# Order of the early loads and of two weight sums in a QKV projection by seven products

## The chip, the cores and the metric

The kernel runs on one core of a Trainium2 chip. The metric is the device time of one execution in microseconds, as the median over runs. TensorE (PE) multiplies, VectorE (DVE), ScalarE (ACT) and GpSimd (POOL) prepare operands and take results out of the PSUM banks, and SyncE (SP) and ACT issue the DMAs between HBM and SBUF.

## The reference

```python
batch, seq, hidden = 16, 512, 768
x: (16, 512, 768) float32          w_qkv: (768, 2304) float32

qkv = np.matmul(x, w_qkv)
q = qkv[..., :hidden]
k = qkv[..., hidden:2*hidden]
v = qkv[..., 2*hidden:]
return np.stack([q, k, v], axis=0).astype(np.float32)
```

So it is one product of 8192 x 768 by 768 x 2304, with its columns stored as three arrays.

## The kernel before

**Tiling.** The rows of x are taken in 32 pairs of two tiles of 128 rows, numbered from 0 ("pair 2" is the third). The 768 contracted elements are six slices of 128, in two halves of three. Of the 2304 columns, q = 0 covers the first 1024 in two blocks of 512 (c = 0, 1), q = 1 the last 1024 in the same way, and between them lies a remainder of 256. "Block (q, c)" is such a block of 512 columns of w; it is loaded in two halves of three slices (768 KB each).

**Two ways to multiply.** Pairs 0 and 1 are done plainly by `block` (L384): for each of four row tiles six bf16 products of 128x512 accumulate in a PSUM bank, and ACT evicts it (L408). Later pairs use, for each q, seven products on 2x2 blocks with sums of operands: `do(u, n)` (L220) does product n of the quad u = (pair, q); its matrix products stand in `product` (L201, matmuls at L212). Products 1 and 2 are bf16, on x itself; the others are f32, on sums. The sums of x are s (`sums_x`, L177, GpSimd) and the sums of w are t1 to t4 (`sum_w(q, n)`, L105, DVE instruction at L113): 6 uses t2, 5 uses t1, 7 uses t3, 4 uses t4, and 3 uses a rounded copy b22. A quad has a bank u.x for products 1, 6, 7 and 4 in turn, evicted by ACT after each (L226, L233, L239, L243), a bank u.z for 2 (added by DVE, L230), and a bank u.y for 5 and then 3 on top of it; DVE adds u.y to one quarter of the result after 5 and 7 (L240) and, with 3 in it, to another (L246). The remainder is plain: `rem` (L267, matmuls L262, eviction L272, store L273).

**Pair 2 is the transition.** For q = 0 it uses the seven products, for q = 1 the plain blocks, because the sums of w for q = 1 aren't ready: its tiles 4 and 5 of blocks (1, 0) and (1, 1) stand between the products of quad a = (2, 0). From pair 3 on, `two` (L275) interleaves two quads. The kernel has a schedule written by hand: every engine executes its instructions in the order of the program text.

**How x arrives.** For pairs 2 and later `load_group` (L124, DMA at L128) fetches a quarter, 192 KB; `load_x` (L119) issues four, two of them on SP and two on the queue given. DVE transposes the pair (`transpose`, L130, instruction at L132) into xf. From xf, ACT rounds pair 2 to bf16 by halves (`round_half`, L470, instruction at L472) and GpSimd later pairs (`round_x`, L173, L175); then GpSimd builds the sums s. There are three buffers for a loaded pair, two for xf, five for a quad's results and eight PSUM banks, each in rotation.

**The early loads.** SP issues, in this order: x of pairs 0 and 1, the blocks of w (0,0), remainder, (0,1), (1,0), (1,1) and two quarters of x of pair 2 (L363 to L367). Stores follow on the same queue when their results are evicted: the remainders (L273), then the quads of pairs 0 and 1 (L253, L254 for q = 0; L257, L258 for q = 1). ACT issues the other two quarters of pair 2 after block (0, 1) (L461). SP gets to x of pair 3 (L463) after the stores of the quads of q = 0. During each plain block ACT casts the next block's two halves (L380) between its evictions.

**The order around the change**, from block (1, 0) on:

```python
    block(1, 0, b1[1], halves(range(4)), cast_next(1, 1, bt1))
    load_x(3, nc.sync)
    ...
    sum_w(1, 1)
    transpose(2)
    ...
    block(1, 1, bt1, halves(range(4)), round_half)
    sums_x(2)
    transpose(3)
    round_x(3)
    sums_x(3)
    sum_w(1, 2)
```

Pair 2 follows (L480 to L498), with `b22[0]` (ACT, L483), sum 3 (L486) and sum 4 (L497). `t_1`, which holds t1 to t4 of q = 1, lies in the buffers of the loaded blocks (0, 0) and (0, 1); t3 and t4 take that of (0, 1), from which `b22[0]` is cast.

Of the kernel before, what the change touches and what calls it, by code (L numbers as in the profile page):

```python
# [10 lines left out]
def kernel(  # L11
# [20 lines left out]
    nc = tc.nc  # L32
    P = 128
# [6 lines left out]
    KH = KT // 2  # L40
    KC = K // 4
    NP = M // (2 * P)
    CB = 512
    REM = N3 - 4 * CB
    Q_OFF = (0, 2 * CB + REM)
    R_OFF = 2 * CB
    fp32 = mybir.dt.float32
    f32r = mybir.dt.float32r
    bf16 = mybir.dt.bfloat16
    ident = mybir.ActivationFunctionType.Identity  # L50
# [12 lines left out]
    st_pool = ctx.enter_context(tc.tile_pool(name="st", bufs=4))  # L63
# [15 lines left out]
    b22 = [w_pool.tile([P, KH, CB], f32r, name=f"b22_{q}") for q in range(2)]  # L79
# [7 lines left out]
    def load_w(dst, j0, nj, off, cols):  # L87
        rows = w_qkv.rearrange("(p j) n -> p j n", j=KT)
        nc.sync.dma_start(dst, rows[:, j0:j0 + nj, off:off + cols])  # L89

    stage = {}

    def load_blocks(q, c, nj=KH):
        if q == 0:
            t = tq_pool.tile([P, KT, CB], fp32, name="st0", tag="tq")
            for j in range(0, KT, nj):
                load_w(t[:, j:j + nj], j, nj, Q_OFF[q] + c * CB, CB)
            stage[q, 0, c], stage[q, 1, c] = t[:, :KH, :], t[:, KH:, :]
        else:
            for h in range(2):  # L100
                t = st_pool.tile([P, KH, CB], fp32, name="st1", tag="st")
                load_w(t[:], h * KH, KH, Q_OFF[q] + c * CB, CB)
                stage[q, h, c] = t[:]

    def sum_w(q, n):  # L105
        t1, t2, t3, t4 = ts[q]
        o, in0, in1 = {
            1: (t1, stage[q, 0, 1], stage[q, 0, 0]),
            2: (t2, stage[q, 1, 1], t1),
            3: (t3, stage[q, 1, 1], stage[q, 0, 1]),  # L110
            4: (t4, stage[q, 1, 0], t2),
        }[n]
        nc.vector.tensor_tensor(o, in0, in1, op=sub)  # L113
# [5 lines left out]
    def load_x(p, other):  # L119
        for n in range(2):  # L120
            for h in range(2):
                load_group(p, 2 * h + n, (nc.sync, other)[h])

    def load_group(p, i, eng):  # L124
        if p not in xin:
            xin[p] = xin_pool.tile([P, 2 * P // G, KC], fp32, name="xin")
        rows = x_flat[p * 2 * P:(p + 1) * 2 * P, :].rearrange("(g b) k -> b g k", b=G)
        eng.dma_start(xin[p][i * G:(i + 1) * G], rows[:, :, i * KC:(i + 1) * KC])  # L128
# [65 lines left out]
    def quad(p, q):  # L194
        u = Quad()
        u.p, u.q = p, q
        u.o = o_pool.tile([P, 2, 2 * CB], fp32, name="o", tag="o")
        u.x = u.y = u.z = None
        return u

    def product(u, n, ps, start):  # L201
        t1, t2, t3, t4 = ts[u.q]
        if n <= 2:
            h = (n - 1) * KH
            lhs = [xb[u.p][:, h + j, :P] for j in range(KH)]
            rhs = [b1[u.q][:, h + j, :] for j in range(KH)]
        else:
            k, t = {3: (4, b22[u.q][:]), 4: (0, t4), 5: (1, t1), 6: (2, t2), 7: (3, t3)}[n]
            lhs = [sr[u.p][:, k, j, :] for j in range(KH)]
            rhs = [t[:, j, :] for j in range(KH)]  # L210
        for j in range(KH):
            nc.tensor.matmul(  # L212
                ps[:], lhs[j], rhs[j],
                start=(start and j == 0), stop=(j == KH - 1), skip_group_check=True,
            )

    def bank():
        return ps_pool.tile([P, CB], fp32, name="ps")

    def do(u, n):  # L220
        c11, c12 = u.o[:, 0, :CB], u.o[:, 0, CB:]
        c21, c22 = u.o[:, 1, :CB], u.o[:, 1, CB:]
        if n == 1:
            u.x = bank()
            product(u, 1, u.x, True)
            nc.scalar.activation(c11, u.x[:], ident)  # L226
        elif n == 2:
            u.z = bank()
            product(u, 2, u.z, True)
            nc.vector.tensor_tensor(c11, c11, u.z[:], op=add)  # L230
        elif n == 6:
            product(u, 6, u.x, False)
            nc.scalar.activation(c12, u.x[:], ident)  # L233
        elif n == 5:
            u.y = bank()
            product(u, 5, u.y, True)
        elif n == 7:
            product(u, 7, u.x, False)
            nc.scalar.activation(c22, u.x[:], ident)  # L239
            nc.vector.tensor_tensor(c22, c22, u.y[:], op=add)  # L240
        elif n == 4:
            product(u, 4, u.x, False)
            nc.scalar.activation(c21, u.x[:], ident)  # L243
        elif n == 3:
            product(u, 3, u.y, False)
            nc.vector.tensor_tensor(c12, c12, u.y[:], op=add)  # L246

    def rows_of(s, p, lo, hi):
        return out_flat[s, p * 2 * P:(p + 1) * 2 * P, lo:hi].rearrange("(r m) n -> m r n", m=P)

    def store_quad(u):
        if u.q == 0:
            nc.sync.dma_start(rows_of(0, u.p, 0, H), u.o[:, :, :H])  # L253
            nc.sync.dma_start(rows_of(1, u.p, 0, 2 * CB - H), u.o[:, :, H:])  # L254
        else:
            part = 2 * H - Q_OFF[1]
            nc.sync.dma_start(rows_of(1, u.p, H - part, H), u.o[:, :, :part])  # L257
            nc.sync.dma_start(rows_of(2, u.p, 0, H), u.o[:, :, part:])  # L258
# [8 lines left out]
    def rem(p):  # L267
        ps = ps_pool.tile([P, 2, REM], fp32, name="ps")
        for r in range(2):
            rem_row(p, r, ps[:, r, :])  # L270
        o = or_pool.tile([P, 2, REM], fp32, name="orem")
        nc.scalar.activation(o[:], ps[:], ident)  # L272
        nc.sync.dma_start(rows_of(1, p, R_OFF - H, R_OFF - H + REM), o[:])  # L273
# [87 lines left out]
    for h in range(2):  # L361
        load_w(st_rem[:, h * KH:(h + 1) * KH], h * KH, KH, R_OFF, REM)
    load_blocks(0, 1, KH)  # L363
    load_blocks(1, 0)
    load_blocks(1, 1)
    for i in range(2):
        load_group(2, i, nc.sync)  # L367
    quads = [[quad(p, q) for p in range(NS)] for q in range(2)]

    def busy(n):  # L370
# [13 lines left out]
    def block(q, c, w, groups, cast_next):  # L384

        ps = {}
        for group in groups:
            if callable(group):  # L390
                group()
                continue
            js, tiles = group
            for n in tiles:
                p, r = divmod(n, 2)
                if n not in ps:
                    ps[n] = bank()
                for j in js:
                    nc.tensor.matmul(
                        ps[n][:], xb[p][:, j, r * P:(r + 1) * P], w[:, j, :],  # L400
                        start=(j == 0), stop=(j == KT - 1), skip_group_check=True,
                    )
                if KT - 1 not in js:
                    continue
                if r == 0:
                    cast_next(p)
                u = quads[q][p]
                nc.scalar.activation(u.o[:, r, c * CB:(c + 1) * CB], ps[n][:], ident)  # L408
                if c == 1 and r == 1:
                    store_quad(u)  # L410

    def halves(tiles):
        return [(range(h * KH, (h + 1) * KH), tiles) for h in range(2)]

    act, dve = nc.scalar, nc.vector
    def cast_next(q, c, w):
        return lambda p: p < 2 and cast(q, p, c, w, act)
# [39 lines left out]
    for n in range(1, 5):  # L457
        sum_w(0, n)
    block(0, 1, bt0, halves(range(4)), cast_next(1, 0, b1[1]))
    for i in range(2, 4):  # L460
        load_group(2, i, act)  # L461
    block(1, 0, b1[1], halves(range(4)), cast_next(1, 1, bt1))
    load_x(3, nc.sync)  # L463
    t_1 = [tq_pool.tile([P, 2, KH, CB], f32r, name=f"t_1{n}", tag="tq") for n in range(2)]
    ts[1] = [t_1[n // 2][:, n % 2] for n in range(4)]
    sum_w(1, 1)
# [13 lines left out]
    a = quad(2, 0)  # L480
    quads[1].append(quad(2, 1))
    do(a, 1)
    act.activation(b22[0][:], stage[0, 1, 1], ident)  # L483
    do(a, 2)
    rem(2)
    sum_w(1, 3)  # L486
    block(1, 0, b1[1], [(range(KT), (4, )), (range(KT), (5, ))], nothing)
    load_x(4, nc.sync)
    do(a, 6)
    do(a, 5)  # L490
    block(1, 1, bt1, [(range(KT), (4, ))], nothing)
    do(a, 7)
# [1 line left out]
    do(a, 4)  # L494
    do(a, 3)
    store_quad(a)
    sum_w(1, 4)  # L497
    act.activation(b22[1][:], stage[1, 1, 1], ident)  # L498

# [43 lines left out]
```

## Time and profile before

| | |
|---|---|
| median of 8 runs | 364.37 us (364.23 to 366.02) |
| the profiled execution | 364.35 us |
| its span, first to last instruction | 362.6 us |
| granted TensorE clock | 0.999 |
| TensorE busy | 352.3 us (97%) |
| DVE, ACT, POOL busy | 224.0, 186.4, 178.8 us |
| HBM traffic | 297 GB/s over the span |

The profile lists instructions by engine with the program's line, the result and the operands ("xf<-xin"), the count where equal ones are merged, and in brackets the idle time before them with what ended it. Starts are measured; the ends of matmuls are modelled, so a matmul's duration is best read from the distance of two starts. In the chain of waits, the work that ended last is followed back from the end; "DMA xin<-in_x_dram" there is the time from the issue of a load to its landing. All times are in us from the first instruction.

### The profile page before, as it was taken

How to read it: one execution, taken by the hardware profiler on the slowest of the kernel's cores; microseconds unless marked ns; L12 is line 12 of the kernel's file. 1: busy time of each engine (PE TensorE's matmuls, PEld its weight loads, DVE VectorE, ACT ScalarE, POOL GpSimd, SP SyncE). 2: the span in 40 equal slices, each digit the busy share in tenths (PEclk: the TensorE clock that was granted, in tenths of full speed). 3: DMA queues.
4: the chain of work that ended last, by engine and by line, in shares of the span. 5: the costliest groups of instructions: out<-in, count | busy, mean ns of one | idle time of the engine just before them, and what ended most of it. 6: DMA issues, size and time to landing. Idle time of an engine off the chain costs nothing.

```text
span 362.6 us, 5205 instructions
## 1 busy us (share of the span) xinstructions
PE 352.3 (97%) x1750; PEld 250.8 (69%) x1782; DVE 224.0 (62%) x233; ACT 186.4 (51%) x308; POOL 178.8 (49%) x185
## 2 busy tenths in 40 slices
PE   8998989999999999999999999999999999999995
PEld 4544467777777777777777777777777777777774
DVE  3583887655666755656765566765566675556643
ACT  4585754554545454454555454545454545554543
POOL 0003677466644456654446664445664445665420
PEclk9999999999999999999999999999999999999999
DMA  7999987888999999999999898898999999999867
GB/s 299 403 374 354 357 292 247 271 302 271 324 304 294 278 294 278 310 307 293 293 273 295 281 324 305 293 272 296 275 323 302 290 288 283 287 294 315 294 235 256
DMA packets 81450, 108.09 MB, mean 298 GB/s; under 512 B 4880, under 2 KB 61456, under 8 KB 81424
## 3 DMA queue, kind: packets, MB, share of 16 engines
q1 hardware_dynamic: 65472, 95.96, 81.0%
q10 hardware_dynamic: 15952, 11.80, 9.9%
q8 instruction: 14, 0.23, 0.3%
q14 instruction: 12, 0.10, 0.1%
HBM read 32.24 MB, written 75.50 MB: 297 GB/s over the span
## 4 chain that ended last, share of the span: by engine, by line
PE 85%; DMA 9%; issue 2%; DVE 1%; SPq 1%; ACT 1%; ACTq 0%; DVEq 0%
PE ps L212 75%; PE ps L262 10%; DMA st<-in_w_qkv_dram 5%; DMA xin<-in_x_dram 4%; DVE t L113 1%; SPq L128 1%; SPq L89 0%; ACT o L243 0%; ACTq L303 0%; SPq L143 0%; ACT b L380 0%; ACT orem L317 0%; DVE o L240 0%; DVE o L230 0%; ACTq L319 0%
## 5 line engine op out<-in xcount | busy, mean ns | idle before, releaser
L212 PE MATMUL ps<-t,s 128*128 128x512 f32 x708 | 177.7, 399 | 0.0
L212 PEld LDWEIGHTS ps<-t,s 128*128 128x128 f32 x708 | 133.0, 188 | 30.4
L175 POOL CAST xb<-xf 128x1536 bf16<-128x1536 f32 x29 | 43.8, 1510 | 133.2 <-DVE xf L132 133.2
L240 DVE TENSOR_TENSOR o<-o,ps 128x512 f32<-128x512 f32 x59 | 40.5, 687 | 91.1 <-ACT o L239 91.1
L132 DVE STREAM_TRANSPOSE xf<-xin 128x1536 f32<-128x1536 f32 x30 | 88.6, 2954 | 8.7 <-DMA xin<-in_x_dram 8.7
L212 PE MATMUL ps<-b,xb 128*128 128x512 bf16 x326 | 80.0, 379 | 3.2 <-ACT xb L472 1.2
L212 PEld LDWEIGHTS <-xb 128*128 128x128 bf16 x354 | 32.1, 98 | 38.1 <-issue 7.6
L239 ACT ACTIVATE o<-ps 128x512 f32<-128x512 f32 x59 | 35.3, 598 | 44.4 <-PE ps L212 44.3
L233 ACT ACTIVATE o<-ps 128x512 f32<-128x512 f32 x59 | 35.3, 598 | 42.2 <-PE ps L212 39.3
L246 DVE TENSOR_TENSOR o<-o,ps 128x512 f32<-128x512 f32 x59 | 40.5, 687 | 22.6 <-PE ps L212 21.4
L212 PE MATMUL ps<-b,s 128*128 128x512 f32 x177 | 49.6, 389 | 1.7 <-DVE o L240 1.7
L226 ACT ACTIVATE o<-ps 128x512 f32<-128x512 f32 x59 | 35.2, 597 | 25.1 <-DVE o L246 21.4
L243 ACT ACTIVATE o<-ps 128x512 f32<-128x512 f32 x59 | 35.3, 598 | 24.2 <-PE ps L212 21.3
L183 POOL TENSOR_TENSOR s<-xf 128x384 fp32r<-128x384 f32 x30 | 31.8, 1061 | 31.7 <-DVE xf L132 31.7
L262 PE MATMUL ps<-w_rem,xb 128*128 128x256 bf16 x384 | 47.2, 273 | 0.0
L262 PEld LDWEIGHTS <-xb 128*128 128x128 bf16 x384 | 37.4, 98 | 11.2 <-issue 0.5
L212 PEld LDWEIGHTS ps<-b,s 128*128 128x128 f32 x177 | 33.1, 188 | 9.0 <-issue 2.1
L230 DVE TENSOR_TENSOR o<-o,ps 128x512 f32<-128x512 f32 x59 | 37.2, 672 | 2.0 <-ACT o L226 1.3
L184 POOL TENSOR_TENSOR s<-s,xf 128x384 fp32r<-128x384 f32 x30 | 30.4, 1013 | 2.4
L187 POOL TENSOR_TENSOR s<-xf,s 128x384 fp32r<-128x384 f32 x30 | 30.4, 1013 | 0.0
L185 POOL TENSOR_TENSOR s<-xf 128x384 fp32r<-128x384 f32 x30 | 30.4, 1012 | 0.0
L272 ACT ACTIVATE orem<-ps 128x512 f32<-128x512 f32 x31 | 18.5, 598 | 20.1 <-PE ps L262 20.1
(35 smaller groups left out, 119.7 us busy)
## 6 DMA issues: line engine op xcount, KB each, us to landing
out_dram<-o SPq DMA_DIRECT2D x62, 768.0 KB, 4.6
out_dram<-o SPq DMA_DIRECT2D x65, 256.0 KB, 4.2
xin<-in_x_dram SPq DMA_DIRECT2D x64, 192.0 KB, 6.9
xin<-in_x_dram ACTq DMA_DIRECT2D x56, 192.0 KB, 4.5
out_dram<-orem SPq DMA_DIRECT2D x31, 256.0 KB, 5.8
st<-in_w_qkv_dram SPq DMA_DIRECT2D x6, 768.0 KB, 11.1
xin<-in_x_dram SPq DMA_DIRECT2D x2, 768.0 KB, 4.9
st<-in_w_qkv_dram SPq DMA_DIRECT2D x6, 256.0 KB, 6.0
```

Source lines behind the costliest of these rows:

```text
L132: nc.vector.transpose(t[:].rearrange("p j (g b) -> p g j b", b=G), xin.pop(p)[:].rearrange("p g (a j) -> p g j a", a=G),)
L175: nc.gpsimd.tensor_copy(out=xb[p][:], in_=xf[p][:])
L183: g.tensor_tensor(s[:, 1], a21, a22, op=add)
L212: nc.tensor.matmul(ps[:], lhs[j], rhs[j], start=(start and j == 0), stop=(j == KH - 1), skip_group_check=True,)
L226: nc.scalar.activation(c11, u.x[:], ident)
L230: nc.vector.tensor_tensor(c11, c11, u.z[:], op=add)
L233: nc.scalar.activation(c12, u.x[:], ident)
L239: nc.scalar.activation(c22, u.x[:], ident)
L240: nc.vector.tensor_tensor(c22, c22, u.y[:], op=add)
L243: nc.scalar.activation(c21, u.x[:], ident)
L246: nc.vector.tensor_tensor(c12, c12, u.y[:], op=add)
L262: nc.tensor.matmul(ps, xb[p][:, j, r * P:(r + 1) * P], w_rem[j // KH][:, j % KH, :], start=(j == 0), stop=(j == KT - 1), skip_group_check= ...
```

## The change

Three things are reordered; nothing is computed differently and no DMA changes its size.

- On SP, the four quarters of x of pair 2 come after the first half of block (1, 1) and ahead of its last half, all four on SP; the two that ACT issued are gone from ACT. The four quarters of pair 3 follow the last half of w, ahead of all stores.
- On DVE, sum 3 of q = 1 goes from its place ahead of pair 2's additions L240 and L246 to behind them, next to sum 4 and ahead of the transpose of pair 4. (Sum 4 keeps its place.)
- On ACT, the cast to `b22[0]` goes from behind product 1 of pair 2 to behind its product 6.

```diff
             for h in range(2):
-                t = st_pool.tile([P, KH, CB], fp32, name="st1", tag="st")
-                load_w(t[:], h * KH, KH, Q_OFF[q] + c * CB, CB)
-                stage[q, h, c] = t[:]
+                load_half(q, h, c)
+
+    def load_half(q, h, c):
+        t = st_pool.tile([P, KH, CB], fp32, name="st1", tag="st")
+        load_w(t[:], h * KH, KH, Q_OFF[q] + c * CB, CB)
+        stage[q, h, c] = t[:]
...
     load_blocks(1, 0)
-    load_blocks(1, 1)
-    for i in range(2):
-        load_group(2, i, nc.sync)
+    load_half(1, 0, 1)
+    load_x(2, nc.sync)
+    load_half(1, 1, 1)
+    load_x(3, nc.sync)
...
     block(0, 1, bt0, halves(range(4)), cast_next(1, 0, b1[1]))
-    for i in range(2, 4):
-        load_group(2, i, act)
     block(1, 0, b1[1], halves(range(4)), cast_next(1, 1, bt1))
-    load_x(3, nc.sync)
...
     do(a, 1)
-    act.activation(b22[0][:], stage[0, 1, 1], ident)
     do(a, 2)
     rem(2)
-    sum_w(1, 3)
     block(1, 0, b1[1], [(range(KT), (4, )), (range(KT), (5, ))], nothing)
     load_x(4, nc.sync)
     do(a, 6)
+    act.activation(b22[0][:], stage[0, 1, 1], ident)
     do(a, 5)
...
     store_quad(a)
+    sum_w(1, 3)
     sum_w(1, 4)
     act.activation(b22[1][:], stage[1, 1, 1], ident)
```

## The prediction

> **What bounds the kernel now.** First the engine table: TensorE is the bound of the whole.
>
> ```profile
> PE 352.3 (97%) x1750; PEld 250.8 (69%) x1782; DVE 224.0 (62%) x233; ACT 186.4 (51%) x308; POOL 178.8 (49%) x185
> ```
>
> So only TensorE's idle time can be won. I asked the waits of PE between 26 and 60 us, where the change lies, and then the timeline of PE there:
>
> ```profile
> PE ps L212 <- DVE o L240: 1.7, 1, 1.7
> PE ps L212 <- ACT xb L472: 1.2, 1, 1.2
> ```
> ```profile
> 27.19 5.34 PE L399 MATMUL ps<-bt,xb 128*128 128x512 bf16 x23
> 33.77 1.47 PE L212 MATMUL ps<-b,xb 128*128 128x512 bf16 x6 [1.24 <-ACT xb L472]
> 46.23 0.93 PE L212 MATMUL ps<-b,s 128*128 128x512 f32 x3 [1.70 <-DVE o L240]
> 47.00 1.47 PE L212 MATMUL ps<-b,xb 128*128 128x512 bf16 x6
> 57.98 1.24 PE L212 MATMUL ps<-b,xb 128*128 128x512 bf16 x5
> ```
>
> Ends are modelled, so I go by starts. The plain products take 0.216 us each (24 from 22.01 to 27.19), the f32 ones 0.227 (three in 0.68), a remainder of 12 is 1.31. Block (1,1), started at 27.19, could hand over at 27.19 + 5.18 = 32.37; pair 2 starts at 33.77: **1.40 lost**, waiting for its rounded x. Pair 2 with its two extra tiles is 30 x 0.216 + 1.31 + 15 x 0.227 = 11.19, so pair 3 could start at 44.96; it starts at 47.00: **2.04 lost**. Pair 3 lasts 10.76 (its successor's first record is missing, so 57.98 less 0.22 = 57.76), like every later pair (10.74). So 3.4 us is all there is.
>
> Who makes them late: the chain of waits, then DVE's timeline.
>
> ```profile
> 22.65 7.06 DMA xin<-in_x_dram
> 32.06 5.68 DMA xin<-in_x_dram
> 40.81 1.73 DVE t L113
> 42.54 0.60 DVE o L230
> 43.14 2.34 DVE t L113
> 45.48 0.61 DVE o L240
> ```
> ```profile
> 29.90 2.93 DVE L132 STREAM_TRANSPOSE xf<-xin 128x1536 f32<-128x1536 f32 x1 [3.69 <-DMA xin<-in_x_dram]
> 37.87 3.03 DVE L132 STREAM_TRANSPOSE xf<-xin 128x1536 f32<-128x1536 f32 x1 [5.03 <-DMA xin<-in_x_dram]
> ```
>
> Both losses begin with x. Pair 2's x lands at 29.7, is transposed to 32.83, rounded to 33.7. Pair 3's lands at 37.8, because its loads sit on SP behind four stores (SP reaches them at 29.77); DVE then waits 5 us with pair 2's sums behind that transpose, and the additions of L230 and L240 behind those sums. L240 must finish before do(a, 3) may add to the same bank.
>
> **The change, part by part.**
>
> *x of pair 2 ahead of the last half block of w.* Four loads of 192 KB now follow the first half of block (1,1), which lands at 23.7 (SP's L253 waits for it until its issue at 23.71). The DMA engines are full, so bytes set the time:
>
> ```profile
> 13.50:18.50 5.00, 5.00 (x37) 3.41 (x35) 2.80 (x3) 3.27 (x7) 0.00 (x0) 1.00 1.05 407
> 42.50:45.00 2.50, 2.03 (x10) 0.96 (x7) 2.50 (x3) 1.63 (x3) 2.50 (x2) 1.00 1.06 279
> ```
>
> These windows end in DMA share and GB/s: 2 KB packets of w move 407 GB/s, a stretch of x and other packets under 2 KB only 279. One pair of x is 786 KB, 2.82 us at 279 (1.93 at 407), so it lands near 23.7 + 2.8 = 26.5, not 29.7. DVE is done with sum 1 at 26.2; the transpose runs 26.6 to 29.6. The first loss's old cause is gone.
>
> *What is late next: the last half of w.* It landed at 26.40 (SP's L254 waits for it until then), and ACT casts it (1.48 us, L380). Now 786 KB of x go first. From below, 23.7 + 1.93 + 1.93 = 27.6; from above, 26.40 + 2.82 = 29.2. I take 28.8, between 23.7 + 2.82 + 1.93 = 28.5 and 29.2: w keeps its speed, but in the old run this half took 2.7 us beside some x. The cast then ends at 30.30, and TensorE, which needs this half for the second twelve products of block (1,1) at 27.19 + 2.59 = 29.78, waits to 30.36 (0.06 from ACT's end to PE's start, as at 33.71 to 33.77). **New stall: 0.58** (0 to 1.0 by the two ends). Queued behind this cast on ACT are two evictions (1.08), the rounding of pair 2's x (0.84) and four more: rounding ends at about 32.3, before pair 2 starts at 32.37 + 0.58 = 32.95; the second half of the rounding is at 34.2, needed at 34.9. The evictions free their banks in time.
>
> [...]
>
> *x of pair 3 ahead of all stores.* Issued behind that half: 28.8 + 2.82 = 31.6, against 37.8. DVE: transpose 31.6 to 34.6, sum 2 to 36.4 (1.73, or 2.34 beside GpSimd's work), L230 at once. GpSimd rounds and sums pair 3 about 6 us earlier. The 5 us idle of DVE goes.
>
> *The stores, later by that.* 1.57 MB go ahead. Quad (0,0)'s store must land before ACT evicts tile 4 into its buffer. It landed at 32.7; remainder and store bytes ahead are the same and 786 KB more x, so 35.5 at most, needed at 32.95 + 1.30 + 1.31 + 1.30 = 36.9. Cost 0, cover 1.4. The loads of pair 4 have the same bytes ahead as before, so they land near 46 as before; DVE wants them at 48.
>
> *Waits of the queues.* SP issues a DMA when the one eight before it has landed (its waits name the DMAs of st and xin). Pair 3's last load so waits for pair 2's first, near 24.5, and the first stores behind it for loads until 29; over 1 MB stays queued meanwhile, so the engines don't run dry. In pair 3, ACT's two loads for pair 5 wait in the same way for quad (2,1)'s first store, near 47 (46.8 before); behind them on ACT stand the remainder's eviction and L233, wanted by 50. Cost 0; without that cover it would be the excess, us for us.
>
> *ACT's two loads and the moved cast.* ACT loses 1.27 us of issuing (22.21). The cast into b22[0] (1.51) stands behind do(a, 6) now, at 39.6 to 41.1; do(a, 3) needs it at 43.5. Cost 0, cover 2.4.
>
> *Sums 3 and 4 behind pair 2's store.* L240 no longer waits for sum 3. Pair 2 runs unhindered from 32.95 to 44.14, the second loss is gone, too. But the two sums now stand ahead of pair 4's transpose and of pair 3's additions. From pair 2's end e: L246 starts at e + 0.2 (47.00 to 47.20) and takes 0.6, two sums 1.72 each, transpose 2.88, two L230 1.2, L240 0.69, 0.15 to PE (46.08 to 46.23): e + 9.16. In a steady pair do(a, 3) comes 8.65 after the start. **New stall 0.51** in pair 3. Inside it hides another: pair 3's first bank is, by eight in rotation, pair 2's x bank, which ACT (L243, 0.60, started 0.24 after the product) lets go 0.3 after e. Together 0.51; with both sums at 2.34 beside GpSimd it would be 1.7; as GpSimd should be done with pair 3 by 43, I take 0.51.
>
> *Sum.* Lost before 1.40 + 2.04 = 3.44; lost after 0.58 + 0.51 = 1.09, and 0.02 as pair 3 had lasted 10.76. Gain 3.46 - 1.09 = 2.37. Later pairs have one period, set by TensorE, and the end is the same. The profiled execution took 364.35, its span 362.6 with 1.75 around it, and the median is 364.37, so the same: 364.35 - 2.37 = 361.98, given as 362.0.
>
> **The rivals.** *All of it is covered:* w lands by 28.2, as at 407 GB/s, and no new stall appears in block (1,1): 364.35 - 2.95 = 361.4 (361.0 if DVE's chain is short, too). For it: 2 KB packets do 407. Against: x has never done so here.
>
> *The stall only moves to w:* the last half lands at 29.8 to 30.9, as small packets slow w as well (786 KB in its old 2.7 us is 292 GB/s): stall 1.6 to 2.7, gain 1.4 to 0.3, some 363.3.
>
> *Nothing measurable:* the new stalls eat what was won, 364.3: w at about 31, or sums slowed by GpSimd and w at 30.
>
> *Slower, by w alone:* each us that the last half of w is late past 28.2 delays all that follows, since nothing behind it has slack to TensorE. From 28.2 + 2.95 = 31.2 on, the time is above today's; at 32.2 it is 365.3. For it, that half stands behind four loads in one queue. Against, 786 KB would need 5 us, 160 GB/s; the slowest full window of 2.5 us here has 279.
>
> **How the numbers follow.** Forecast 0.52, all covered 0.15, moved to w 0.15, nothing 0.09, slower 0.09. About 0.2%, or 0.7 us, is what a measurement of this kernel tells from no change. Faster: 0.52 + 0.15 + 0.15 = 0.82; same 0.09; slower 0.09. The range goes from the short-chain case, 361.0, over the moved stall to its bad end, 363.8; it leaves out the last two cases.
>
> **What would show it.** Right: pair 2's transpose starts before 28; PE has a wait of some 0.6 us in block (1,1) on ACT's cast, none at pair 2's start, one of some 0.5 us on L240 or L243 about pair 3; pair 4 starts near 55.4 in place of 57.76. Wrong in size: the cast ends after 31.3, or DVE's sums 3 and 4 take over 2 us. Wrong in kind: PE waits in pair 2, or for an eviction held by a store, or a later pair lasts more than 10.74.

## The result and the profile after

The changed kernel takes **367.15 us** (median of 11 runs, 365.40 to 368.64) against 364.39 for the kernel before in the same comparison: ratio **1.0070, 95% interval 1.0055 to 1.0085**. It is slower by 2.6 us (by the ratio; 2.8 between the medians) where 2.4 us less were forecast. The profiled execution took 367.31, with a span of 365.5 and a mean granted clock of 0.995. In the changed kernel's text the lines named before stand 3 to 4 lower: the plain matmuls are L403, their cast L384, the seven products L215, the transpose L135, the sums of w L116, the additions L233, L243 and L249.

TensorE's row of the engine table, the waits of PE between 15 and 62 us, and PE's timeline there (start, duration, line, count; in brackets the wait and what ended it):

```profile
PE 354.1 (97%) x1750; PEld 251.6 (69%) x1782; DVE 222.8 (61%) x233; ACT 187.0 (51%) x308; POOL 175.7 (48%) x185
```
```profile
PE ps L403 <- ACT bt L384: 3.7, 1, 3.7
PE ps L215 <- DVE o L243: 0.3, 1, 0.3
```
```profile
27.41 2.75 PE L403 MATMUL ps<-bt,xb 128*128 128x512 bf16 x12
33.88 0.84 PE L403 MATMUL ps<-bt,xb 128*128 128x512 bf16 x3 [3.71 <-ACT bt L384]
34.94 3.37 PE L403 MATMUL ps<-bt,xb 128*128 128x512 bf16 x8 [0.22 <-issue]
38.15 1.46 PE L215 MATMUL ps<-b,xb 128*128 128x512 bf16 x6
49.43 1.47 PE L215 MATMUL ps<-b,xb 128*128 128x512 bf16 x6
...
58.54 0.94 PE L215 MATMUL ps<-b,s 128*128 128x512 f32 x3 [0.25 <-DVE o L243]
...
60.94 1.24 PE L215 MATMUL ps<-b,xb 128*128 128x512 bf16 x5
```

Both old losses are gone: nothing waits for rounded x at 38.15, where pair 2 starts, and nothing in pair 2 for L243, the old L240. In their place stands one wait in the middle of block (1,1), before its second twelve products: they could have started at 27.41 + 2.59 = 30.00 and start at 33.88, a stall of **3.88 us** where 0.58 was forecast. The chain of waits names who is late:

```profile
18.78 13.54 DMA st<-in_w_qkv_dram
32.32 0.02 issue
32.34 1.49 ACT bt L384
33.83 0.04 issue
33.88 0.84 PE ps L403 x3
```

The last half of w, issued at 18.78, lands at 32.32. Forecast was 28.8. A second cost stands in the windows of the changed kernel (stretch, length, busy time and count of PE, PEld, DVE, ACT, POOL, then granted clock, DMA share and GB/s):

```profile
22.50:24.50 2.00, 2.00 (x11) 0.93 (x10) 1.96 (x2) 1.92 (x3) 0.00 (x0) 1.00 1.12 235
28.50:30.50 2.00, 1.67 (x8) 0.68 (x7) 1.64 (x1) 0.00 (x0) 0.00 (x0) 1.00 1.11 239
35.00:36.50 1.50, 1.50 (x4) 0.53 (x4) 1.50 (x1) 1.48 (x3) 1.39 (x2) 0.50 1.04 412
```

After the wait the clock is granted at 0.50: from 33.88 to 38.15 the twelve products take 4.27 us instead of 2.59, **1.68 more**. And in the two stretches in which x of pairs 2 and 3 is moved, the DMA engines are busy all the time (share over 1) and yet move only 235 and 239 GB/s.

DVE's timeline has the transposes of pairs 2 and 3, each early, and L243 of pair 2 without a sum ahead of it:

```profile
28.86 2.90 DVE L135 STREAM_TRANSPOSE xf<-xin 128x1536 f32<-128x1536 f32 x1 [1.33 <-DMA xin<-in_x_dram]
34.28 2.98 DVE L135 STREAM_TRANSPOSE xf<-xin 128x1536 f32<-128x1536 f32 x1 [2.51 <-DMA xin<-in_x_dram]
...
47.56 0.69 DVE L243 TENSOR_TENSOR o<-o,ps 128x512 f32<-128x512 f32 x1 [7.16 <-ACT o L242]
```

**The account.** Pair 4's first record is missing, so it starts at 60.94 - 0.22 = 60.72, against 57.76 before: 2.96 later, and 367.31 - 364.35 is 2.96. Of it: the stall 3.88, the clock 1.68, pair 3 longer by 0.53 (60.72 - 49.43 = 11.29 against 10.76), pair 2 by 0.09 (11.28 against 11.19) and block (1,1) starting 0.22 later, 6.40 in all; off it go the old losses of 1.40 and 2.04. What remains is 2.96.

### The profile page after: what moved, and what is told of

Same layout as the page of the kernel before. It is cut to its first block, busy times and chain, and to the rows that moved or that the text cites. A ratio compares the mean times of both kernels' runs of the same rounds, so it can differ in the third digit from the quotient of the medians.

```text
span 365.5 us, 5202 instructions
## 1 busy us (share of the span) xinstructions
PE 354.1 (97%) x1750; PEld 251.6 (69%) x1782; DVE 222.8 (61%) x233; ACT 187.0 (51%) x308; POOL 175.7 (48%) x185
## 4 chain that ended last, share of the span: by engine, by line
PE 86%; DMA 5%; SPq 3%; DVE 2%; ACT 1%; issue 1%; ACTq 0%
PE ps L215 74%; PE ps L265 10%; DMA st<-in_w_qkv_dram 5%; PE ps L403 3%; SPq L131 2%; SPq L89 1%; DVE xf L135 1%; DVE t L116 0%; ACT bt L384 0%; ACT o L246 0%; ACTq L306 0%; DVE o L233 0%; SPq L146 0%; ACT orem L320 0%; DVE o L243 0%
## 5 line engine op out<-in xcount | busy, mean ns | idle before, releaser
L215 PE MATMUL ps<-t,s 128*128 128x512 f32 x708 | 177.7, 399 | 0.0
L215 PEld LDWEIGHTS ps<-t,s 128*128 128x128 f32 x708 | 133.0, 188 | 30.5
L243 DVE TENSOR_TENSOR o<-o,ps 128x512 f32<-128x512 f32 x59 | 40.4, 686 | 97.2 <-ACT o L242 97.2
L135 DVE STREAM_TRANSPOSE xf<-xin 128x1536 f32<-128x1536 f32 x30 | 88.6, 2953 | 3.8 <-DMA xin<-in_x_dram 3.8
L215 PE MATMUL ps<-b,xb 128*128 128x512 bf16 x326 | 80.0, 379 | 1.9
L215 PEld LDWEIGHTS <-xb 128*128 128x128 bf16 x354 | 32.2, 98 | 36.7 <-issue 7.9
L249 DVE TENSOR_TENSOR o<-o,ps 128x512 f32<-128x512 f32 x59 | 40.5, 687 | 23.3 <-PE ps L215 22.2
L215 PE MATMUL ps<-b,s 128*128 128x512 f32 x177 | 49.7, 390 | 0.3 <-DVE o L243 0.3
L246 ACT ACTIVATE o<-ps 128x512 f32<-128x512 f32 x59 | 35.3, 598 | 24.8 <-PE ps L215 21.8
L186 POOL TENSOR_TENSOR s<-xf 128x384 fp32r<-128x384 f32 x30 | 30.3, 1009 | 30.6 <-DVE xf L135 30.6
L233 DVE TENSOR_TENSOR o<-o,ps 128x512 f32<-128x512 f32 x59 | 37.1, 671 | 2.8 <-ACT o L229 2.1
L215 PEld LDWEIGHTS ps<-b,s 128*128 128x128 f32 x177 | 33.1, 188 | 7.5 <-POOL xb L178 0.6
L188 POOL TENSOR_TENSOR s<-xf 128x384 fp32r<-128x384 f32 x30 | 30.3, 1011 | 0.0
```

What stands on the lines that cost most here:

```text
L135: nc.vector.transpose(t[:].rearrange("p j (g b) -> p g j b", b=G), xin.pop(p)[:].rearrange("p g (a j) -> p g j a", a=G),)
L215: nc.tensor.matmul(ps[:], lhs[j], rhs[j], start=(start and j == 0), stop=(j == KH - 1), skip_group_check=True,)
```

## The experiments

Two theories stood against each other. A: the loads cost the time, since w's last half comes late behind x; in its strict form, x of pair 3 right behind that half slows it further. B: the two moved sums cost it. Later it was asked why the half is so late. All ratios are against the kernel before, run beside each kernel. Where no range is given, there was one execution.

### Each part alone

**Loads only** (e1): the changed kernel with the sums and the cast back in their old places.

```diff
     do(a, 1)
+    act.activation(b22[0][:], stage[0, 1, 1], ident)
     do(a, 2)
     rem(2)
+    sum_w(1, 3)
...
-    act.activation(b22[0][:], stage[0, 1, 1], ident)
...
-    sum_w(1, 3)
     sum_w(1, 4)
```

> The changed loads with the two sums and the cast into b22[0] in their old places. Theory A (the loss is all in the loads: the last half of w lands at 32.3 and TensorE then waits 3.9 us and runs slow for 1.7): the same stall as in the changed kernel, 3.5 to 4.1 us in block (1,1), and pair 3 loses its 0.5 us, since only sum 4 stands ahead of pair 4's transpose: 366.3 to 366.9. Theory B (the later sums cost the time): about the time before, 364.4, or less.

366.93 us (366.72 to 367.23), ratio 1.0062 [1.0047, 1.0077]. PE's timeline has the same wait:

```profile
34.30 4.00 PE L403 MATMUL ps<-bt,xb 128*128 128x512 bf16 x12 [4.08 <-ACT bt L384]
```

This lies at the upper end of what theory A gave (366.3 to 366.9): the loads alone make the kernel slower; theory B falls. Pair 3 takes 10.74 here (49.86 to 60.60), so the moved sums are what costs the 0.5 us in pair 3.

**Sums only** (e2): the loads of before, sum 3 and the cast in their late places (the diff is against the changed kernel).

```diff
-    load_half(1, 0, 1)
-    load_x(2, nc.sync)
-    load_half(1, 1, 1)
-    load_x(3, nc.sync)
+    load_blocks(1, 1)
+    for i in range(2):
+        load_group(2, i, nc.sync)
...
+    for i in range(2, 4):
+        load_group(2, i, act)
     block(1, 0, b1[1], halves(range(4)), cast_next(1, 1, bt1))
+    load_x(3, nc.sync)
```

> The old loads with sum 3 and the cast into b22[0] in their new places. Theory A: pair 2's start stays at 33.8 (its x lands at 29.7 as before), but L240 no longer stands behind sum 3, so pair 2 ends 1.7 to 2.0 us earlier, and 0.5 us is given back in pair 3 by the two sums ahead of the transpose: 362.8 to 363.2. Theory B: slower than before, 364.9 or more.

364.04 us (363.81 to 364.54), ratio 0.9981 [0.9971, 0.9992]: a gain, but a smaller one than the expected 362.8 to 363.2. Pair 3 starts at 45.10, 1.9 earlier than before, as expected, and then loses most of it:

```profile
55.22 0.93 PE L212 MATMUL ps<-b,s 128*128 128x512 f32 x3 [1.25 <-DVE o L240]
```

With x of pair 3 still late, GpSimd works on it while DVE does the two sums, and they take 1.88 and 2.55 us instead of 1.75 each, and the wait is 1.25. It is the case for which the prediction had named a price of 1.7 and not taken it.

### Where the loads stand

**x behind w** (e3): both halves of block (1,1) first, then x of pairs 2 and 3, all on SP.

```diff
     load_half(1, 0, 1)
-    load_x(2, nc.sync)
     load_half(1, 1, 1)
+    load_x(2, nc.sync)
     load_x(3, nc.sync)
```

> The changed kernel with both halves of block (1,1) ahead of x of pair 2; x of pairs 2 and 3 then follow on SP ahead of all stores, and the sums are late. Theory A (the half is late because x's packets go beside it): the last half lands by 26.4 as before, no stall in block (1,1), full clock; x of pair 2 lands at 28.5 to 30, pair 2 starts at 32.5 to 33.8, pair 3 loses 0.5: 361.8 to 363.2. If a long queue on SP alone makes the loads late, whatever their order: the half lands after 28 and the time is 364 or more.

363.54 us (363.12 to 365.33), ratio 0.9974 [0.9958, 0.9991]. There is no wait in block (1,1), as expected; x of pair 2 lands late instead, at 30.48 where 28.5 to 30 was expected, and the time lies 0.3 above its range:

```profile
34.45 1.47 PE L215 MATMUL ps<-b,xb 128*128 128x512 bf16 x6 [2.02 <-ACT xb L473]
```

**x of pair 3 in its old place** (e4): x of pair 2 still between the halves.

```diff
     load_half(1, 1, 1)
-    load_x(3, nc.sync)
...
     block(1, 0, b1[1], halves(range(4)), cast_next(1, 1, bt1))
+    load_x(3, nc.sync)
```

> The changed kernel with x of pair 3 loaded after the first stores, as before; x of pair 2 stays between the halves. Theory A in its strict form (the piece of w on the last DMA engine is slowed by x's small packets that run beside it on the others, x of pair 3 among them): the half lands 1 to 1.5 us earlier, at 30.8 to 31.3, and the stall is 2.4 to 2.9. If only the bytes ahead of the half count, x of pair 3 behind it is nothing to it: it lands at 32.3 again and the stall is 3.9.

364.78 us (364.44 to 365.10), ratio 1.0004 [0.9994, 1.0013]. The wait in block (1,1) falls to less than half:

```profile
31.48 2.75 PE L402 MATMUL ps<-bt,xb 128*128 128x512 bf16 x12 [1.72 <-ACT bt L383]
```

The same half in the same place behind the same loads lands at 29.92 instead of 32.32. What came **after** it in the queue had slowed it: theory A in its strict form, and by more than it had put (a landing at 30.8 to 31.3). The time gains less than that, since pair 3 loses 1.40 us here, as its x is late and the two sums take 2.08 and 2.55 us, as in e2:

```profile
55.72 0.93 PE L215 MATMUL ps<-b,s 128*128 128x512 f32 x3 [1.40 <-DVE o L243]
```

### What a late part of a load is

The trace has 16 updates of a semaphore for each load. In the changed kernel 15 of those of w's last half are in at 28.84 and the last at 32.32, and the cast that waits for the half starts at 32.34, so it is the last one that counts. Each update is taken here as the part of one of the 16 DMA engines; the table shows the end of the last of 15 and that of the slowest, in us. The records don't name the engine; that the slowest part is always that of one and the same engine is inferred from the lag, which goes on from load to load.

| kernel | first half of (1,1) | x of pair 2 | last half of (1,1) |
|---|---|---|---|
| before | 22.37 / 23.65 | 29.13 / 29.71 | 24.60 / 26.38 |
| changed | 22.69 / 25.65 | 26.18 / 28.67 | 28.84 / 32.32 |
| x of pair 3 in its old place (e4) | 22.82 / 25.39 | 26.10 / 28.33 | 28.57 / 29.92 |
| short packets into 128 partitions (e6) | 22.41 / 23.71 | 24.54 / 25.82 | 26.52 / 27.74 |
| short packets into 64 partitions (e10) | 22.69 / 25.77 | 26.11 / 28.68 | 28.83 / 32.12 |
| pair 1's plain products left out (e7) | 22.68 / 22.86 | 25.97 / 26.07 | 28.26 / 29.34 |
| x behind w (e3) | 22.47 / 23.88 | 28.15 / 30.48 | 24.68 / 27.49 |
| w, x of pair 2, a store, x of pair 3 (e16) | 22.46 / 23.87 | 28.09 / 29.30 | 24.66 / 27.44 |
| x of pair 3 early (e9) | 22.40 / 23.85 | 30.22 / 31.17 | 24.66 / 27.32 |

In the changed kernel 15 engines had the last half in at 28.84, the forecast's 28.8. One had it 3.48 later. The first load with a late part is the one ahead of these, the last half of block (1, 0), at 20.47 / 21.94. At 18.67 us, while it was in flight, a transfer begins that is not the program's; the DMA view between 18 and 20 us has it among the rows of packets, MB and share by queue:

```profile
q8 instruction: 1, 0.02, 3.0%
```

It is 16 KB of instructions in a single packet, which took 0.96 us. The same fetch is in the kernel before (at 18.60, 0.94 us).

**Long packets** (e5): x of pairs 2 and 3 as 128 packets of 1536 bytes into 128 partitions for each load, the same bytes of x in another arrangement, so what pairs 2 and 3 multiply is other data.

```diff
+        if p in (2, 3):
+            rows = x_flat[p * 2 * P:(p + 1) * 2 * P, :].rearrange("(r m) k -> m r k", m=P)
+            r, c = divmod(i, 2)
+            wide = xin[p][:].rearrange("m g k -> m (g k)")
+            eng.dma_start(wide[:, i * 2 * KC:(i + 1) * 2 * KC], rows[:, r, c * 2 * KC:(c + 1) * 2 * KC])
+            return
```

> The changed kernel, but the eight early loads of x (pairs 2 and 3) fetch their 192 KB each as 128 packets of 1536 B into all 128 partitions instead of 256 packets of 768 B into 32; the elements of these two pairs therefore stand in other places, and their results are of other data. Same bytes, same number of DMAs, same order. Theory A (x's small packets slow the w packets of the DMA engine that lags): x of pair 2 takes about 2 us, the lagging engine keeps 84 ns a packet of 2 KB, the last half of w lands at 27.5 to 28.5 in place of 32.3, the wait in block (1,1) is under 0.5 us, the time 361.5 to 362.5. If the bytes alone or the long queue make it late: it lands after 31, 366 to 367.

361.31 us; no wait in block (1,1). This changes two things at once, the packet and the partitions, so the next kernel holds the packet.

**Short packets into 128 partitions** (e6): the same 768 bytes as in the changed kernel, two for each of 128 partitions; other data again.

```diff
+        if p in (2, 3):
+            rows = x_flat[p * 2 * P:(p + 1) * 2 * P, :].rearrange("(r m) k -> m r k", m=P)
+            eng.dma_start(xin[p][:, 2 * i:2 * i + 2], rows[:, :, i * KC:(i + 1) * KC])
+            return
```

> As the changed kernel, with each early load of x as 256 packets of 768 B from the very same rows, but into all 128 partitions instead of 32 (two slots of each; the elements stand in other places, so pairs 2 and 3 are of other data). If the packets' size is what slows the others: lands at 32 as in the changed kernel, near 367. If it is that a load goes to 32 partitions: as with long packets, lands at 27.5 to 29.0, 361.5 to 362.8.

361.38 us, as with long packets. The windows view, same columns as above:

```profile
22.50:24.50 2.00, 2.00 (x11) 0.94 (x10) 1.98 (x2) 2.00 (x4) 0.00 (x0) 1.00 1.09 383
```

383 GB/s with packets of the size that moved 235 before. Some packets of w are in this stretch, too; by the table the four loads of x of pair 2 take 15 engines 2.13 us (22.41 to 24.54) against 3.49 in the changed kernel (22.69 to 26.18). So packet size, my explanation until then, falls: the 32 partitions that one load of x goes to are what slows it. The table shows both effects: the 15 engines are done with w's last half 2.3 us earlier (26.52 against 28.84), and the late one stays 1.2 us behind throughout, where in the changed kernel it falls 3.5 us behind.

**Short packets into 64 partitions** (e10): the same again, with 64 adjacent partitions for each load (other data).

```diff
+        if p in (2, 3):
+            rows = x_flat[p * 2 * P:(p + 1) * 2 * P, :].rearrange("(g b) k -> b g k", b=2 * G)
+            lo, g0 = (i // 2) * 2 * G, (i % 2) * 4
+            eng.dma_start(
+                xin[p][lo:lo + 2 * G, g0:g0 + 4], rows[:, :, i * KC:(i + 1) * KC]
+            )
+            return
```

> The changed kernel, with the early loads of x of pairs 2 and 3 taken as packets of the same 768 bytes and the same number, but into 64 adjacent partitions for each load in place of 32 (what lies in each partition is other data of x). Loads into 128 partitions gave 361.4, into 32 give 367.2. If the number of partitions is what counts, 64 lie between: x packets near 45 ns, the last half of w near 30, 363 to 365. If 64 adjacent partitions are no better than 32, the last half of w lands near 32 again and the time is 366 to 367.5. [...]

367.12 us, last half at 32.12, and in the windows view:

```profile
22.50:24.50 2.00, 2.00 (x11) 0.94 (x10) 1.94 (x2) 1.90 (x3) 0.00 (x0) 1.00 1.11 239
```

Twice the partitions bring nothing: 239 GB/s against 235, and 3.42 us for x of pair 2 on 15 engines against 3.49. The second of the two expectations held. In the changed kernel x alone, 737 KB on 15 engines in 3.49 us, ran at 211; the 235 of the window holds packets of w from the late engine as well.

**Pair 1's plain products left out** (e7): the plain blocks and the remainder of pair 1 are not computed, so that the fetch of instructions falls at another time.

```diff
...
-    for p in range(2):
-        rem(p)
+    rem(0)
...
-    block(0, 1, bt0, halves(range(4)), cast_next(1, 0, b1[1]))
-    block(1, 0, b1[1], halves(range(4)), cast_next(1, 1, bt1))
+    block(0, 1, bt0, halves(range(2)), cast_next(1, 0, b1[1]))
+    block(1, 0, b1[1], halves(range(2)), cast_next(1, 1, bt1))
...
-    block(1, 1, bt1, halves(range(4)), round_half)
+    block(1, 1, bt1, halves(range(2)), round_half)
```

> The changed kernel without the plain products, evictions and stores of pair 1 (its results are not written). The loads stay as they are. TensorE's instructions before block (1,1) are fewer by about a hundred, so the fetch of its next 16 KB of instructions, at 18.4 to 18.7 us in every run so far, comes some ten us later. If that fetch is what makes one DMA engine lag: no half of w lands with a straggler before it, the first half of block (1,1) lands at 22.7 in place of 25.7 and the last half at 28.2 to 29.0 in place of 32.3. If the straggler has another cause: 25.7 and 32.3 again. The time itself says nothing here.

364.44 us (not to be compared, as work is left out). The fetch is at 26.90 instead of 18.67. The first half of (1,1) then lands with no late engine, 22.86, and the last one has a late part again, born at 26.9: the lag follows the fetch of instructions.

**x by rows** (e13): the true data into their true places, but as eight loads for each pair, each with one packet for each of the 128 partitions; and the same with the sums in their old places (e14).

```diff
+        if p in (2, 3):
+            xin[p] = xin_pool.tile([P, 2 * P // G, KC], fp32, name="xin")
+            for g in range(2 * P // G):
+                r0 = p * 2 * P + g * G
+                nc.sync.dma_start(
+                    xin[p][:, g],
+                    x_flat[r0:r0 + G, :].rearrange("b (i k) -> i b k", k=KC),
+                )
+            return
```

> The changed kernel with the same data of x in the same places of SBUF, but the loads of pairs 2 and 3 cut otherwise: in place of four loads of 256 packets into 32 partitions, eight loads of 128 packets of the same 768 bytes, one packet into each of the 128 partitions. If it is the 32 (or 64) adjacent partitions of one load that slow x and starve the late DMA engine, x packets take 36 ns again, the last half of w lands near 27.7, TensorE doesn't wait in block (1,1), and the time is that of the short packets into 128 partitions, 361.4 (361.2 to 361.8). If the earlier gain came from the other order of the data in those kernels, or if eight smaller loads cost time in the queue (SP issues a load when the one eight before has landed), the last half lands at 29 or later and the time is 362.5 to 367.

> As the kernel with x of pairs 2 and 3 loaded by rows into 128 partitions, but sum 3 and the cast to b22 in their old places (changed loads only). Pair 3 lost 0.53 us by the late sums in the changed kernel, nothing in the kernel with the changed loads only. If that holds where nothing else is late, this is 0.5 us below its sister: 360.9 (360.7 to 361.3). If sum 3 ahead of the additions of pair 2 makes TensorE wait there, it is level with its sister or above it.

370.87 us (370.52 to 371.96), ratio 1.0176 [1.0162, 1.0190], and 370.58 (370.26 to 372.10), 1.0159 [1.0145, 1.0173]: both misses, and worse than all others. In the windows view:

```profile
24.00:26.00 2.00, 2.00 (x11) 0.93 (x10) 1.97 (x2) 2.00 (x3) 0.00 (x0) 1.00 0.27 93
```

A DMA share of 0.27, about 4 of 16 engines, moves 93 GB/s, where the stretches with x of the changed kernel had shares of 1.12 and 1.11. The load's source has an outermost dimension of 4; that this is the cause was not shown. With so much of the DMA engines idle, these kernels say nothing on partitions with the true data, and e14 against e13 (0.3 us with ranges that overlap) doesn't settle the sums either.

### The clock

**The wait filled** (e8): 17 matmuls on zeros between the halves of block (1,1), so that TensorE isn't idle while it waits.

```diff
-    block(1, 1, bt1, halves(range(4)), round_half)
+    first, second = halves(range(4))
+    block(1, 1, bt1, [first, lambda: busy(17), second], round_half)
```

> The changed kernel with 17 products of zeros (3.7 us) in the wait of block (1,1) before its second half, into a bank of their own. If the granted clock falls because TensorE stands still for 3.9 us: the second half runs at full clock, 2.6 us in place of 4.3, and the time falls by 1.3 to 1.7 to 365.4 to 365.9. If the clock falls for another reason, or the lower clock costs nothing: 367.0 to 367.5.

365.69 us (365.18 to 366.14), ratio 1.0023 [1.0010, 1.0037] against the changed kernel's 1.0070: by doing more work, 0.47% or 1.7 us less (1.5 between the medians). In PE's timeline the second twelve products run from 33.62 to 36.21, 2.59, at full speed:

```profile
29.90 3.83 PE L378 MATMUL ps<-zero 128*128 128x512 bf16 x17
33.62 2.75 PE L403 MATMUL ps<-bt,xb 128*128 128x512 bf16 x12
36.21 1.46 PE L215 MATMUL ps<-b,xb 128*128 128x512 bf16 x6
```

So of the changed kernel's loss 1.5 to 1.7 us is the clock, not the wait itself. Its own executions say the same: the two with a mean granted clock of 0.999 took 365.40, the others, at 0.991 to 0.995, 366.51 to 368.64.

### Other orders

**x of pair 3 early, nothing ahead of w** (e9), and the same with late sums (e11): the kernel before with one load moved.

```diff
     for i in range(2):
         load_group(2, i, nc.sync)
+    load_x(3, nc.sync)
...
-    load_x(3, nc.sync)
```

> The kernel before with one edit: x of pair 3 on SP right behind SP's two quarters of pair 2, ahead of all stores; no load goes ahead of w, and the sums and the cast to b22 stay in their old places. If the slow last half of w is what costs the changed kernel its time, w lands here as before (about 26.4), TensorE doesn't wait in block (1,1), the first loss of 1.4 us stays, the second of 2.0 goes, and pair 3 loses nothing since sum 3 is in its old place: 364.35 - 2.04 = 362.3 (362.2 to 363.0). Rival: x of pair 3 takes bandwidth from the two quarters of pair 2 on ACT's queue, and pair 2 starts up to 1 us later: 363.3.

> As the kernel with only x of pair 3 early, but with sum 3 and the cast to b22 in their late places. In the changed kernel pair 3 lost 0.53 us by them, with old loads 1.25. With pair 3's x early GpSimd is done early, so 0.5 us: 362.8, 0.4 to 0.6 above its sister in this call. If the late sums help by freeing pair 2's additions, it is at or below its sister: 362.3 or less.

365.54 us (363.93 to 366.05), ratio 1.0008 [0.9991, 1.0025], and 365.76 (364.69 to 366.70), 1.0019 [1.0006, 1.0033]. For e9 the rival held and still fell 2.2 short. No x stood ahead of w, and TensorE didn't wait for w, though its last half landed at 27.32 instead of 26.38; but x of pair 2 now had x of pair 3 right behind it on the other queue, landed at 31.17 instead of 29.71, and after a wait of 2.82 us the clock was granted at 0.50:

```profile
35.20 2.60 PE L212 MATMUL ps<-b,xb 128*128 128x512 bf16 x6 [2.82 <-ACT xb L472]
```
```profile
35.50:37.50 2.00, 2.00 (x6) 0.72 (x5) 2.00 (x2) 2.00 (x5) 1.97 (x3) 0.50 1.03 393
```

So x of pair 3 hurts not only w. By the table most of it is not the late engine here: the other 15 had x of pair 2 at 30.22 instead of 29.13, so of the 1.46 us 1.1 is the DMA engines' time shared with x of pair 3, as the rival said, and 0.4 the lag. Late sums cost 0.2 us between the medians, but these mix executions in which the clock fell (9 of 11 in e9, 6 of 11 in e11, with a mean clock of 0.995 or less) with others in which it didn't. Like with like, e11 is 0.4 above e9 where the clock fell (medians 366.00 and 365.56) and 0.7 where it didn't (364.82 and 364.08, five executions and two): about the 0.4 to 0.6 expected.

**ACT's quarters early** (e12): as e9, and ACT issues its two quarters of pair 2 ahead of its cast of the remainder's w; SP's loads of (1,0), (1,1), two quarters of pair 2 and pair 3 follow there in the text.

```diff
-    load_blocks(1, 0)
-    load_blocks(1, 1)
-    for i in range(2):
-        load_group(2, i, nc.sync)
...
+        for i in range(2, 4):
+            load_group(2, i, act)
+        load_blocks(1, 0)
+        load_blocks(1, 1)
+        for i in range(2):
+            load_group(2, i, nc.sync)
+        load_x(3, nc.sync)
         act.activation(w_rem[1][:], st_rem[:, KH:], ident)
...
-    for i in range(2, 4):
-        load_group(2, i, act)
...
-    load_x(3, nc.sync)
```

> As the kernel with only x of pair 3 early, and besides ACT issues its two quarters of pair 2 some 11 us earlier, ahead of its cast of the remainder's w, so that they share the DMA engines with w. If pair 2's x lands before 27 and w of (1,0) and (1,1) isn't late, both losses go: 364.35 - 3.4 = 361.0, up to 361.6. If the loads into 32 partitions slow w also here, the halves of (1,0) or (1,1) come late and TensorE waits in those blocks, 1 us or more: 362.3 to 364.

363.24 us (363.09 to 363.41), ratio 0.9958 [0.9943, 0.9973]. The second case held: TensorE waits 1.12 us for a cast of block (1,0) and 0.77 for x of pair 2.

**A store between the two pairs of x** (e16), and the same with the old loads of pair 2 (e17): x of pair 3 is issued between the stores of quad (0,0) and those of quad (1,0). In e16 all of pair 2's x follows block (1,1) on SP as well:

```diff
     load_blocks(1, 1)
-    for i in range(2):
-        load_group(2, i, nc.sync)
+    load_x(2, nc.sync)
...
                 if c == 1 and r == 1:
                     store_quad(u)
+                    if (q, p) == (0, 0):
+                        load_x(3, nc.sync)
...
-    for i in range(2, 4):
-        load_group(2, i, act)
...
-    load_x(3, nc.sync)
```

> The kernel before with two edits: all four quarters of pair 2 on SP behind both halves of block (1,1), and x of pair 3 between the two stores of quad (0,0) and those of quad (1,0). No x goes ahead of w, and no x of pair 3 stands right behind pair 2's, so that the late DMA engine gets through its share of pair 2 while the others move stores. If x into 32 partitions on the other 15 engines is what starves the late engine, pair 2's x lands at 28.5 to 29.7 instead of 30.5 (x of pair 3 right behind), pair 2 starts 4.1 later at 32.6 to 33.8 (loss 0.2 to 1.4), and pair 3's x lands by 34, which takes the second loss: 361.1 to 362.3. Rival: the late engine lags as far beside stores, x of pair 2 lands at 30.5 again and pair 2 starts at 34.5: 363 or more.

> The kernel before with one edit: x of pair 3 between the stores of quad (0,0) and those of quad (1,0), instead of behind both. Pair 2's x lands as before (29.7, two quarters on ACT's queue), so the first loss of 1.4 us stays; pair 3's x lands by 34 instead of 37.8 and the second loss of 2.0 goes: 362.3 (362.0 to 362.8). If x of pair 3 so close behind delays the two quarters on ACT's queue as in the kernel with x of pair 3 ahead of all stores, pair 2 starts near 35 and TensorE's clock halves: 364 to 365.5.

e16: **362.00 us** (361.68 to 362.15), ratio **0.9923 [0.9905, 0.9940]**. e17: 362.46 (362.29 to 362.60), 0.9935 [0.9916, 0.9954]. Both as expected. PE's timeline of e16:

```profile
33.29 1.47 PE L212 MATMUL ps<-b,xb 128*128 128x512 bf16 x6 [0.87 <-ACT xb L470]
...
44.59 1.47 PE L212 MATMUL ps<-b,xb 128*128 128x512 bf16 x6
...
55.55 1.24 PE L212 MATMUL ps<-b,xb 128*128 128x512 bf16 x5
```

One wait of 0.87 remains of the 3.44; pairs 2 and 3 run in 11.30 and 10.74. In e3 and e16 x of pair 2 is in on 15 engines at 28.15 and 28.09; with x of pair 3 behind it the late engine needs until 30.48, with stores behind it until 29.30. So the late engine catches up more slowly beside loads into 32 partitions than beside stores; it is not all the same what the others move. e16 and e17 are the fastest kernels of the study that compute all of the reference.

## Why the prediction was wrong

**The step that failed: the landing of the last half of w, 28.8 (bounds 27.6 to 29.2).** It landed at 32.32, past both bounds. 15 of the 16 DMA engines had it at 28.84; that this is the forecast's 28.8 is luck, as three errors cancel. They were done with the first half at 22.69, not 23.7, then took 3.49 us for x of pair 2 where 2.82 was put, and 2.66 for the half where 2.3 was. The 16th engine was missed altogether. The old landings that I started from, 23.7 and 26.4, already held a lag of 1.3 and 1.8 us, which I took for part of the transfer and for something that stays: in the changed kernel the first half was in at 22.69 on 15 engines and at 25.65 on the last, and beside two pairs of x the lag grew to 3.48. The upper bound, the old 26.40 plus 2.82, could not hold it, since it added x once and the growth of the lag not at all. Going by the slow row, 279 GB/s, was half right: a stretch with x was the right kind of row, and 235 to 239 is what the stretches with little else than x move; the reason I gave in passing, small packets, was wrong (e6).

**The second failed term: the price of a stall.** Each us of lateness was counted as one us; the clock was put at nothing, without a reason. The stall took 3.88 us and 1.68 more at half the clock; e8 shows that term by itself. The stall's excess of 3.30 and these 1.68 are 4.98 of the 5.33 us by which the profiled execution missed 361.98. The rival "slower, by w alone" put 365.3 at a landing of 32.2 by the same counting; with the clock's 1.68 it would have been 367.0. That rival was the case that came. I argued against it with 160 GB/s as the rate it would need. It needed no such rate: 15 engines brought their parts in 2.66 us, and the cast waited for the slowest, at 32.32.

**What I weighed and what I missed.** The row of 279 GB/s was rightly taken for x in place of w's 407, and even so it was too fast: 15 engines took 3.49 us for x of pair 2. What I missed was to ask what makes x slow. By e6 and e10 it is the adjacent partitions that one load goes to: 3.49 us into 32, 3.42 into 64, 2.13 into 128.

**What held.** The second loss is gone, and so is the first one's old cause: pair 2's transpose starts at 28.86 instead of 29.90, later than the 26.6 forecast, as pair 2's x landed at 28.67 and not 26.5; pair 3's at 34.28, forecast 31.6, instead of 37.87. Pair 2 runs in 11.28, with the sums behind it. Pair 3 loses 0.53, forecast 0.51, and by the path that was forecast: its products on L243's bank start 9.11 after pair 2's end (49.43 to 58.54), forecast 9.16. e1 without the late sum 3 loses none. No eviction was held up by a store: the one for which the trace names a store, that of pair 2's remainder at 41.00, starts 0.25 after its products end, the next pair's 0.20. Later pairs kept their period of 10.74. The waits in SP's queue, priced at zero, cost nothing that the trace shows.

**Chances and range.** The half's lateness was one doubt with three cases, 0.15 for moved to w, 0.09 and 0.09 for worse. The range ended at 363.8 because these two were left out; the price of the clock would have lain beyond any of them.

**What stays open.** Why the engine that is behind falls further back. In the changed kernel its lag grows over both halves of w (1.47 to 2.96 and 2.49 to 3.48) and shrinks over both pairs of x (2.96 to 2.49 and 3.48 to 1.93). Its 2 KB packets of the last half take about 150 ns each (24 of them from 28.67 to 32.32), against 84 beside loads into 128 partitions (e6) or stores (e4). Packets of w on other engines are slowed beside x, too: between 24 and 26 us the median of 157 packets is 134 ns in the changed kernel, and 84 in e6. What they wait for the records don't say. Nor does every lag grow: in e7 it was 1.08 at w's last half and fell to 0.47 over x of pair 3 behind it. The kernels that tell partitions from packet size (e5, e6, e10) and the one with the fetch moved (e7) are one execution each and don't compute the reference; none was run that brings the true data of x over 16 engines into 128 partitions in one load.

## What to carry to other kernels

A landing time read from these profiles is that of the slowest of 16 parts (32.32 here, with 15 in at 28.84): look at how far it lags the other 15, and ask what the queue behind it will do to that lag, since the loads *after* the awaited one made it later (32.32 with x of pair 3 behind it, 29.92 without). Loads into few adjacent partitions are best kept away from the time in which something is awaited, with other transfers placed between (here stores: x of pair 2 landed at 29.30 with them behind it, at 30.48 with x of pair 3). And a stall of TensorE of some 3 us is to be priced with the slow clock after it: here 3.9 us of waiting cost 5.6, in 9 of 11 executions.

## What the runs showed of the hardware

- The same 786 KB of x in 768-byte packets took 15 engines 3.49 us into 32 partitions, 3.42 into 64 adjacent ones (e10) and 2.13 into 128 (e6); the windows have 235, 239 and 383 GB/s, all with the DMA engines busy throughout: a DMA share of 1 is no sign of full speed.
- A fetch of 16 KB of instructions took 0.96 us (0.94 in the kernel before), and one part of each load behind it stayed 1.2 us late until 33.8 us where all loads go into 128 partitions (e6); beside loads into 32 or 64 it was 1.9 to 3.5 late (changed, e10).
- TensorE's clock stayed at 1.0 after waits of 1.72 (e4) and 2.02 us (e3) and fell to 0.50 after 2.73 (e11), 2.82 (e9) and 3.71 (changed), and 3.16 us into one of 4.96 (e7). The length alone doesn't decide it: two of the changed kernel's 11 executions kept a mean clock of 0.999, and two of e3's ten had 0.994 and 0.995 (365.16 and 365.33 us). In the traces of the kernels before and after, the clock changes only at whole steps of 3.41 us: before up at 6.74 and down at 361.72 (104 steps), after up at 7.20, down at 34.51 (8 steps) and up at 37.92 (one more). How much of one step is idle may be what counts, by my estimate. In the steps that ended with a fall TensorE stood still for 2.78 us (changed), 2.82 (e9), 2.50 (e11), 2.28 (at 61.63 us in e14) and 2.07 (at 35.64 in e1); after 2.01 (the step before that in e1) and 1.91 (at 61.82 in e13) the clock stayed. Then it would depend on where the steps lie whether the same wait costs the clock. That is argued from the profiled executions, and no run tested it.
- The loads of x by rows (e13) moved 93 GB/s, on a DMA share of 0.27; why so few DMA engines were busy no run shows.
